# One semaphore for both scatters of a buffer, 30 loads in halves, and holes in two more groups of a rank-and-scatter kernel

## Chip, cores, metric

One core of one Trainium2 chip. The metric is the device time of one execution in microseconds (us). The kernel before took 771.68 us at first (median of 3 runs, 771.5 to 772.51). A change counts as faster or slower from 2% on. Chips differ at this size: on some the kernel before took 771 to 798 us. They are called busy below, though what disturbs them is not known, and their runs are marked.

## The reference

```python
B, N, D = 8, 2048, 2560
order = np.argsort(scores, axis=1)
ranks = np.argsort(order, axis=1)
out[b_idx, ranks, :] = x          # float32, each row of 10240 bytes goes to the place of its rank
```

## The kernel before

VectorE counts for each score how many are smaller; that is the rank. The rest is moving 168 MB in and 168 MB out. Each batch has 8 groups of 256 rows. Group 0 of the first six batches is copied row by row from DRAM to DRAM by the two hardware queues, issued from SyncE (SP) and ScalarE (ACT): "hardware rows". The other 58 groups are loaded by GpSimd into one of 8 buffers (128 partitions, two rows each) and written by two indirect scatters, one for each column of rows.

A set of four neighbouring partitions is served by one of the 16 DMA engines. In some groups a set of four is left out (a "hole"): its rank is pushed out of bounds so that the scatter skips it, and its rows go as hardware rows instead. That relieves one engine.

```python
NBUF, LAG, G = 8, 4, 16
DIRECT = range(6)
THIN = {**{(b, 4): 48 for b in range(1, B, 2)}, (7, 5): 44}   # (batch, group): first partition of the hole
THIN_LOADS = [k for k in THIN if k[0]]                         # these loads skip the hole as well
HALVED = range(34)                                             # loads 0..33 are issued as two halves
... # cut
def load(line, k, sem):
    ... # cut: groups of THIN_LOADS use an indirect load that skips the hole
    for j in range(m if k in HALVED else 1):
        part = slice(j * D, (j + 1) * D) if k in HALVED else slice(0, m * D)
        line.eng.dma_start(out=xb[k % NBUF][:, part], in_=rows[:, part]).then_inc(sem, 16)
... # cut
def scatters_done(line, k):
    i = k % NBUF
    for j in range(GROUPS[BULK[k][1]][1]):
        line.wait(s_scat[i][j], 16 * n_scat[i][j])
... # cut
for k, (b, g) in enumerate(BULK):
    if k >= LAG and k + NBUF - LAG < len(BULK):
        scatters_done(pl, k - LAG)
        load_ahead(k + NBUF - LAG)
    pl.wait(*loaded[k])
    pl.after(dve, t_bulk[b, g])
    for j in range(GROUPS[g][1]):
        scatter(k, j)
```

## Time and profile before

| | before |
|---|---|
| span of the profiled execution | 769.8 us |
| HBM read, written | 168.25 MB, 168.18 MB |
| data moved by the DMA engines | 415 GB/s mean |
| scatters, loads issued by GpSimd | 116, 62 halves + 21 whole + 5 with a hole |
| hardware rows | 792 (SP) + 784 (ACT) |
| end of the last 640-byte record on the hardware queues (SP, ACT) | 756.6 and 751.7 us |
| last landing (semaphore increment) of a scatter | 768.6 us |

In the profile's queue lists, q0 is GpSimd's queue, q1 and q10 are those of SP and ACT. The numbers behind a queue are records ("packets"), MB, and the share of 16 engines' time. A hardware row is one record of 640 bytes and one of 4 bytes (the semaphore) on each of the 16 engines.

### The profile page before, as it was taken

Reading aid. Unit: us, or ns where it says so; the run is one execution under the profiler, and the core shown is the slowest. Engines: PE = TensorE matmul, PEld = TensorE weight load, DVE = VectorE, ACT = ScalarE, POOL = GpSimd, SP = SyncE. Lnnn points to the kernel's source line nnn. Section 1 sums busy time; section 2 is a strip of 40 time slices with the busy share of each in tenths; the row PEclk is TensorE's granted clock in tenths of the full one; section 3 lists DMA queues with packets and bytes.
Section 4 is the critical chain, followed back from the end, with each engine's and each line's share of the span. In section 5 each row is a group of like instructions: output and inputs, shape, how many; then the busy total and the mean of one; then the engine's idle time right before and its main releaser. Section 6 shows DMA issues by size and latency. Waiting matters only on the chain.

```text
span 769.8 us, 8160 instructions
## 1 busy us (share of the span) xinstructions
PE 33.4 (4%) x166; PEld 29.2 (4%) x166; DVE 400.1 (52%) x824; ACT 0.0 (0%) x1; POOL 167.1 (22%) x213
## 2 busy tenths in 40 slices
PE   4000020020020020110000000000000000000000
PEld 4000010010010010110000000000000000000000
DVE  5999979999979999899999200000000000000000
ACT  0000000000000000000000000000000000000000
POOL 4114214312213131221212121212112121312100
PEclk8555555555555555565555555555555555555555
DMA  8999999999999999999999999999999999999997
GB/s 356 420 419 418 418 421 417 417 419 419 418 417 417 416 419 417 419 419 418 417 418 418 425 417 423 417 422 419 422 417 423 419 420 422 419 425 416 426 411 332
DMA packets 80130, 319.74 MB, mean 415 GB/s; under 512 B 28580, under 2 KB 53796, under 8 KB 53796
## 3 DMA queue, kind: packets, MB, share of 16 engines
q0 software_dynamic: 29376, 300.66, 92.0%
q1 hardware_dynamic: 25648, 10.85, 5.2%
q10 hardware_dynamic: 25088, 8.08, 4.2%
q14 instruction: 17, 0.14, 0.0%
q8 instruction: 1, 0.02, 0.0%
HBM read 168.25 MB, written 168.18 MB: 437 GB/s over the span
## 4 chain that ended last, share of the span: by engine, by line
DMA 63%; DVE 13%; another core or an unknown queue 10%; POOL 6%; issue 4%; PE 1%; POOLq 0%; SPq 0%
DMA out_dram<-x,rank_i 57%; DVE trash L262 12%; DMA x<-in_x_dram 6%; POOL out_dram L476 4%; POOL x L149 2%; DVE s_all L384 0%; POOL x L135 0%; PE ps_all L219 0%; DMA s_in<-in_scores_dram 0%; PE ps_col L198 0%; DVE rank_i L300 0%; DVE rank L294 0%; DVE rank L288 0%; PE ps_row L323 0%
## 5 line engine op out<-in xcount | busy, mean ns | idle before, releaser
L262 DVE TENSOR_SCALAR_CACHE_REDUCE trash<-s_all,s_col 128x1792 bf16<-128x1792 f32 (+7 forms) x240 | 315.2, 1348 | 4.6
L476 POOL DMA_INDIRECT out_dram<-x,rank_i x116 | 113.4, 978 | 135.8 <-issue 34.3
L149 POOL DMA_DIRECT2D x<-in_x_dram x83 | 46.7, 564 | 393.3 <-DMA out_dram<-x,rank_i 391.3
L262 DVE SCALAR_TENSOR_TENSOR trash<-s_all,s_col,mask 128x256 bf16<-128x256 f32 x128 | 61.5, 481 | 0.0
L219 PE MATMUL ps_all<-ident,s_col 128*128 128x128 f32 x128 | 27.2, 400 | 3.2 <-DVE s_all L384 2.8
L219 PEld LDWEIGHTS ps_all<-ident,s_col 128*128 128x128 f32 x128 | 26.0, 219 | 4.1 <-DVE s_all L384 3.1
L323 PE MATMUL ps_row<-ident,rank 128*1 128x128 f32 x22 | 5.9, 365 | 388.7 <-DVE rank_i L309 281.5
L384 DVE COPY s_all<-ps_all 128x512 f32<-128x512 f32 x32 | 20.6, 687 | 3.2 <-PE ps_all L219 2.8
L262 DVE DVE_READ_ACCUMULATOR trash<-s_all,s_col 128x1 f32 x240 | 19.9, 83 | 0.0
L323 PEld LDWEIGHTS ps_row<-ident,rank 128*1 128x1 f32 x22 | 1.3, 86 | 391.5 <-DVE rank_i L309 282.8
L135 POOL DMA_INDIRECT x<-in_x_dram,thin_row x5 | 5.2, 1031 | 43.9 <-DMA out_dram<-x,rank_i 40.3
L262 DVE DVE_READ_ACCUMULATOR trash<-s_all,s_col,mask 128x1 f32 x128 | 10.7, 83 | 0.0
L334 DVE TENSOR_SCALAR thin_i<-ps_row 1x8 int32<-1x8 f32 x5 | 0.8, 153 | 10.2 <-PE ps_row L323 10.2
L349 DVE TENSOR_SCALAR rows_i<-ps_row 1x256 int32<-1x256 f32 x6 | 2.5, 412 | 4.1 <-PE ps_row L323 4.1
L206 DVE COPY s_col<-ps_col 128x128 f32<-128x128 f32 x1 | 0.3, 292 | 4.5 <-PE ps_col L198 4.5
L198 PE MATMUL ps_col<-ident,s_in 8*128 8x8 f32 x16 | 2.1, 262 | 3.7 <-DMA s_in<-in_scores_dram 3.7
L198 PEld LDWEIGHTS ps_col<-ident,s_in 8*128 8x128 f32 x16 | 2.0, 211 | 3.7 <-DMA s_in<-in_scores_dram 3.7
L300 DVE CAST rank_i<-rank 128x16 int32<-128x16 f32 (+3 forms) x11 | 1.9, 173 | 0.4
L294 DVE TENSOR_TENSOR rank<-rank,acc 128x16 f32<-128x16 f32 (+3 forms) x11 | 1.9, 171 | 0.4
L288 DVE TENSOR_TENSOR rank<-acc,acc 128x16 f32<-128x16 f32 (+3 forms) x11 | 1.9, 170 | 0.4
L309 DVE TENSOR_SCALAR rank_i<-rank,hole 128x2 int32<-128x2 f32 x5 | 1.1, 229 | 0.2
L179 POOL TENSOR_SCALAR_AFFINE_SELECT mask<-mask 128x256 f32<-128x256 f32 x2 | 0.8, 396 | 0.0
(13 smaller groups left out, 2.5 us busy)
## 6 DMA issues: line engine op xcount, KB each, us to landing
x<-in_x_dram POOLq DMA_DIRECT2D x62, 1280.0 KB
x<-in_x_dram POOLq DMA_DIRECT2D x21, 2560.0 KB
out_dram<-in_x_dram SPq DMA_DIRECT2D x792, 10.0 KB
out_dram<-in_x_dram ACTq DMA_DIRECT2D x784, 10.0 KB
x<-in_x_dram SPq DMA_DIRECT2D x2, 1280.0 KB, 9.0
out_dram<-x,rank_i POOLq DMA_INDIRECT x116, 48.3
x<-in_x_dram,thin_row POOLq DMA_INDIRECT x5
s_in<-in_scores_dram SPq DMA_DIRECT2D x1, 64.0 KB
```

The costliest lines, as they stand in the source:

```text
L135: nc.gpsimd.indirect_dma_start(out=xb[k % NBUF][:, :m * D], out_offset=None, in_=x.rearrange("b (q j) d -> (b q) (j d)", j=m), in_offset=b ...
L149: line.eng.dma_start(out=xb[k % NBUF][:, part], in_=rows[:, part]).then_inc(sem, 16)
L198: nc.tensor.transpose(out=ps_col[:, B * c:B * (c + 1)], in_=s_in[:, r + j:r + m * P:m], identity=ident[:B, :B],)
L219: nc.tensor.transpose(out=ps_all[:, P * c:P * (c + 1)], in_=s_col[:, c, b:b + 1].to_broadcast([P, P]), identity=ident[:],)
L262: do(out=trash[i][:, :P * (hi_c - lo_c)], in0=s_all[:, P * lo_c:P * hi_c], accum_out=acc[i][:, col:col + 1], **how,)
L288: nc.vector.tensor_tensor(out=rank[:, cols], in0=acc[0][:, cols], in1=acc[1][:, cols], op=OP.add)
L294: nc.vector.tensor_tensor(out=rank[:, cols], in0=rank[:, cols], in1=acc[2][:, cols], op=OP.add)
L300: nc.vector.tensor_copy(out=rank_i[:, cols], in_=rank[:, cols])
L323: nc.tensor.transpose(out=ps_row[:1, P * j:P * (j + 1)], in_=rank[:, col:col + 1], identity=ident[:],)
L349: nc.vector.tensor_scalar(out=rows_i[b][:].rearrange("o (p j) -> o p j", p=P), in0=ps_row[:1, :WIDE].rearrange("o (j p) -> o p j", p=P), s ...
L384: nc.vector.tensor_copy(out=s_all[:, 512 * q:512 * (q + 1)], in_=ps_all[:, 512 * q:512 * (q + 1)],)
L476: nc.gpsimd.indirect_dma_start(out=out_flat, out_offset=bass.IndirectOffsetOnAxis(ap=rank_i[:, col:col + 1], axis=0), in_=xb[k % NBUF][:, ...
```

## The change

The aim, as the edit suggests it, is balance at the end. Two groups more get a hole: one column of (4,4) skips partitions 48-51, both columns of (6,4) skip 36-39; their loads stay whole. Four loads fewer are cut in halves, and one semaphore counts both scatters of a buffer, which saves half of the waits.

```diff
-    THIN = {**{(b, 4): 48 for b in range(1, B, 2)}, (7, 5): 44}
+    THIN = {(1, 4): 48, (3, 4): 48, (4, 4): 48, (5, 4): 48, (6, 4): 36, (7, 4): 48, (7, 5): 44}
+    THIN_COLS = {k: 1 if k == (4, 4) else 2 for k in THIN}
-    THIN_LOADS = [k for k in THIN if k[0]]
-    HALVED = range(34)
+    THIN_LOADS = [(1, 4), (3, 4), (5, 4), (7, 4), (7, 5)]
+    HALVED = range(30)
...
-        s_scat = [[nc.alloc_semaphore(f"scat{i}_{j}") for j in range(MMAX)] for i in range(NBUF)]
+        s_scat = [nc.alloc_semaphore(f"scat{i}") for i in range(NBUF)]
...
         def scatters_done(line, k):
-            i = k % NBUF
-            for j in range(GROUPS[BULK[k][1]][1]):
-                line.wait(s_scat[i][j], 16 * n_scat[i][j])
+            line.wait(s_scat[k % NBUF], 16 * n_scat[k % NBUF])
... (ranks pushed out of bounds, rows copied and scatters bounds-checked for THIN_COLS columns, not for all)
```

More of the change, by code (lines that the diff above doesn't have):

```diff
@@ L97 @@
     thin_row = pool.tile([P, len(HOLES)], I32, name="thin_row")
-    thin_i = {k: pool.tile([1, 4 * MMAX], I32, name=f"thin_i{k[0]}_{k[1]}") for k in THIN}
+    thin_i = {k: pool.tile([1, 4 * THIN_COLS[k]], I32, name=f"thin_i{k[0]}_{k[1]}") for k in THIN}
     rows_i = {b: pool.tile([1, WIDE], I32, name=f"rows_i{b}") for b in DIRECT}
@@ L117 @@
         s_load = [nc.alloc_semaphore(f"load{i}") for i in range(NBUF)]
-        s_scat = [
-            [nc.alloc_semaphore(f"scat{i}_{j}") for j in range(MMAX)]
-            for i in range(NBUF)
-        ]
+        s_scat = [nc.alloc_semaphore(f"scat{i}") for i in range(NBUF)]
         s_rows = {sp: nc.alloc_semaphore("rows_sp"), act: nc.alloc_semaphore("rows_act")}
-        n_scat = [[0] * MMAX for _ in range(NBUF)]
+        n_scat = [0] * NBUF
         n_load = [0] * NBUF
@@ L304, in ranks @@
                 if (b, g) in THIN:
-                    cols = slice(b * C + first_col(g), b * C + first_col(g + 1))
+                    cols = slice(b * C + first_col(g), b * C + first_col(g) + THIN_COLS[b, g])
                     i = HOLES.index(THIN[b, g])
@@ L330, in thin_to_bytes @@
         def thin_to_bytes(b, g):
-            m = GROUPS[g][1]
+            m = THIN_COLS[b, g]
             dve.after(pe, pe.n)
@@ L420, in thin_rows @@
             )
-            for i in range(4 * m):
+            for i in range(4 * THIN_COLS[b, g]):
                 row = b * N + r + (THIN[b, g] + i % 4) * m + i // 4
@@ L474, in scatter @@
             col = b * C + first_col(g) + j
-            n_scat[k % NBUF][j] += 1
+            n_scat[k % NBUF] += 1
             nc.gpsimd.indirect_dma_start(
@@ L481, in scatter @@
                 element_offset=b * N * D,
-                **(dict(bounds_check=N - 1, oob_is_err=False) if (b, g) in THIN else {}),
-            ).then_inc(s_scat[k % NBUF][j], 16)
+                **(dict(bounds_check=N - 1, oob_is_err=False) if j < THIN_COLS.get((b, g), 0) else {}),
+            ).then_inc(s_scat[k % NBUF], 16)
         def load_ahead(k):
```

## The prediction

> **What bounds the kernel now.** The page comes first, and of it the slices of the span, the DMA queues and the chain.
>
> ```profile
> DVE  5999979999979999899999200000000000000000
> ...
> DMA  8999999999999999999999999999999999999997
> GB/s 356 420 419 418 418 421 417 417 419 419 418 417 417 416 419 417 419 419 418 417 418 418 425 417 423 417 422 419 422 417 423 419 420 422 419 425 416 426 411 332
> ...
> q0 software_dynamic: 29376, 300.66, 92.0%
> q1 hardware_dynamic: 25648, 10.85, 5.2%
> q10 hardware_dynamic: 25088, 8.08, 4.2%
> ...
> DMA 63%; DVE 13%; another core or an unknown queue 10%; POOL 6%; issue 4%; PE 1%; POOLq 0%; SPq 0%
> ```
>
> The DMA engines are busy in every slice but the first and the last. VectorE, which computes the ranks, is done by 428 us, so nothing that it does later can hold the end. The shares of the queues add up to 101.4%: there is no idle time to fill in the middle. Counting the packet records of the trace that are in flight at each moment, I find 16 or more at every sampled moment from 30 to 745 us (mean 16.4 of 16 engines). So each engine works without a pause until its own list is empty, and the kernel ends when the engine with the longest list ends. The waits agree:
>
> ```profile
> POOL x L149 <- DMA out_dram<-x,rank_i: 391.3, 43, 11.1
> ```
>
> GpSimd, which issues the loads and scatters, idles about 10 us of each 13.1 us iteration for a scatter to land, always four iterations behind; its instructions are not the limit. The end is seen in the stretches:
>
> ```profile
> 740.00:750.00 10.00, 0.00 (x0) 0.00 (x0) 0.00 (x0) 0.00 (x0) 0.87 (x1) 0.50 1.02 413
> 750.00:760.00 10.00, 0.00 (x0) 0.00 (x0) 0.00 (x0) 0.00 (x0) 0.00 (x0) 0.50 1.02 424
> 760.00:770.00 10.00, 0.00 (x0) 0.00 (x0) 0.00 (x0) 0.00 (x0) 0.00 (x0) 0.50 0.57 240
> ```
>
> The last two columns are DMA share and GB/s. Until 760 us all engines are full, then they run dry one after the other. How unevenly is told by the 16 semaphore increments of the last scatter in the trace, one from each engine, in us of the span:
>
> ```
> 765.0 765.3 765.4 765.5 765.6 765.6 765.9 765.9 765.9 766.0 766.1 766.2 766.4 766.8 767.6 768.6
> ```
>
> Median 765.9, mean 766.0; one engine (call it B) is 2.7 us late, another (A) 1.7, the third last 0.9. Perfect balance would end at 766.0, which is 2.6 us, or 0.3%, better. That is the most that any rebalancing can give.
>
> **Who A and B are.** I took the same increments for each scatter through the run and the lag of the last two behind the median. With scatter pairs (batch, group) in order, first column of each: (6,4) 5.2 and 5.3; (6,7) 5.3 and 5.9; (7,0) 4.0 and 5.3; (7,1) 2.6 and 3.9; (7,3) 2.5 and 4.5; (7,5) 1.2 and 2.4; (7,7) 1.7 and 2.7. The load of (7,4), which skips partitions 48-51, is queued just ahead of scatter (7,0), and that of (7,5), which skips 44-47, ahead of (7,1). So the engine that falls from 6.3 (second column of (6,7)) to 4.0 is B, served by the hole at 48, and the one that falls from 5.3 to 2.6 a step later is A, served by the hole at 44. B is late by some 0.4 us more in each iteration and is pulled back at each odd batch; A grows to 5.3 us by 430 us and stays there.
>
> **What the Trainium skill says.** "DMA: Bandwidth & Descriptors", section "The descriptor swizzle", gives for a 128-partition transfer engine = 8*(partition>>6) + ((partition>>2)&7): four partitions of a hole belong to one engine, 48 to engine 4, 44 to engine 3, 36 to engine 1. The trace numbers no engines, but it agrees that one hole pulls back just one of 16. Section "Queues, rings and completion order" says that each engine goes round-robin between the queue rows that it has work for; the three busy queues and the absence of gaps agree. Section "Why a DMA increments its semaphore by 16 and not by 1" warns that two DMAs in flight on one semaphore let a partial count mislead. The new code waits only for the full sum of both scatters, so the wait ends at the same landing as the two waits before. Section "Where 436 GB/s comes from" puts the ceiling at 435 GB/s; here 10240 bytes in 385 ns on 16 engines are 426, and the slices show 416 to 426, so nothing but fewer or cheaper packets, or better balance, is left.
>
> **The change, part by part.** Durations are from the packet records of this trace: a 10240-byte packet 386 ns (mean), a 20480-byte one 761 ns, a 640-byte packet 32 ns and its semaphore write 9 ns.
>
> ```profile
> x<-in_x_dram POOLq DMA_DIRECT2D x62, 1280.0 KB
> x<-in_x_dram POOLq DMA_DIRECT2D x21, 2560.0 KB
> out_dram<-in_x_dram SPq DMA_DIRECT2D x792, 10.0 KB
> out_dram<-in_x_dram ACTq DMA_DIRECT2D x784, 10.0 KB
> ```
>
> 1. Halves, 34 to 30. Four loads change from two issues to one: 62 becomes 54, 21 becomes 25. GpSimd saves 4 x 0.56 us of issue, beside its waits: worth 0. On each engine 4 loads x 8 partitions x (2 x 386 - 761 = 11 ns) = 0.35 us, and 4 semaphore writes x 9 ns = 0.04: -0.39 us on every engine.
> 2. Rows by the hardware queues. (4,4) adds 4 rows and (6,4) adds 8: 796 on the first queue, 792 on the second. A row is 16 packets of 640 bytes, one on each engine: 12 x (32 + 9) = +0.49 us on every engine. The two new loads stay whole (they are not in the list of thinned loads), so the skipped rows are now read twice, 0.12 MB in 168.
> 3. Hole at 48 in one column of (4,4): engine B drops 4 packets x 386 = -1.54 us.
> 4. Hole at 36 in both columns of (6,4): its engine drops 8 packets x 386 = -3.09 us. It is neither A nor B by the identification above, so this should not move the end.
> 5. One semaphore for two scatters: one wait instruction less for each buffer's turn, tens of ns on an engine that idles 391 us. Worth 0.
> 6. VectorE: one more reduction for the third hole (0.07 us) and two more pairs of small operations (0.23 us and 0.15 us each), early or done by 428 us: 0.
>
> Sum: an engine without a hole moves by +0.49 - 0.39 = +0.10 us. A ends at 767.6 + 0.1 = 767.7; B at 768.6 + 0.1 - 1.5 = 767.2; the third at 766.9. The last landing goes from 768.6 (B) to 767.7 (A): -0.9 us. The timed result follows one for one: 771.68 - 0.9 = 770.8 us, a ratio of 0.9988.
>
> **Rivals.**
> (a) A takes over at more than its 1.7, or B's gain is eaten. B's lag in the (6,4) to (6,7) stretch stands close to the 5.3 at which A stays flat for 20 iterations. If 5.3 were a ceiling that the hardware sets for any late engine, B would be back at it before the last batch and the 1.5 us would be lost: the end at 768.3 to 768.7, the time 771.4 to 771.8. Against it: B reaches 6.3.
> (b) The hole at 36 does serve one of the late engines, because indirect scatters map partitions otherwise or because I swapped engines. If A gets the 3.1 us, the end is B's, 767.2, or the third's, 766.9: 770.0 to 770.3. The author's choice of 36 speaks for it, the fall of A at the load with the hole at 44 against.
> (c) The longer list of hardware rows becomes the bound. The hardware queues' last packets end at 757.0 and 752.1; at about 0.9 us a row of one queue, four and eight rows more end near 761 and 759, six us ahead of the end. Unlikely; it would show as a tail of 640-byte packets and cost up to 1 us.
> (d) Whole loads give the hardware queues fewer turns. Against it: stretches with whole loads (500 to 700 us) move 420 to 421 GB/s, those with halves (200 to 400 us) 418. Part of that may be VectorE's end, which falls at the same place. If it is all the packets' doing, the gain of point 1 is 0.3 us for four iterations of 13.1 us (0.6%), the size that I have.
>
> **Range and chances.** The sum is -0.9, the rivals span -1.7 to +0.3, and the three runs of before lie 1.0 us apart, so a median can be off by some 0.5. I take 770.8 with 769.8 to 771.9. Two per cent are 15.4 us, six times the whole imbalance: within 2% is all but sure.
>
> **What would show it.** Right: 54 half and 25 whole loads, 796 and 792 rows; last landings with the latest engine 1.5 to 2 us behind the median instead of 2.7; from scatter (4,4) on, B 1.5 us less late than before; the median of the last scatter unchanged within 0.3 us. Wrong: if the late engine of the flat 5.3 drops by 3 at scatter (6,4), the hole at 36 serves A, and rival (b) holds; if B stands as late as before by (6,7), rival (a); if the median itself moved by over 0.5 us, the packet sums miss something, such as a changed rate of the hardware queues.

## The result, and the profile after

772.35 us (median of 4 runs, 771.57 to 772.64) against 771.59 us (4 runs, 771.11 to 772.51) of the kernel before. The ratio is 1.0007, 95% interval 0.999 to 1.0024. (A ratio is the mean time of one kernel's fast runs over that of the other's of the same rounds, so not quite the ratio of the medians.) So nothing measurable came of the change, and the 0.9 us that was predicted did not come. The median lies 0.45 us above the range. A second set (e4 below) gave 771.6 us and ratio 1.0006.

The page of the kernel after, the lines that answer to those of before:

```profile
DMA  8999999999999999999999999999999999999997
GB/s 358 419 419 420 418 419 418 419 418 416 420 416 418 418 411 420 419 418 418 423 418 420 423 416 425 415 427 416 425 416 425 418 424 414 426 415 422 419 414 311
...
q0 software_dynamic: 28800, 300.54, 91.9%
q1 hardware_dynamic: 25776, 10.89, 5.2%
q10 hardware_dynamic: 25344, 8.16, 4.2%
...
x<-in_x_dram POOLq DMA_DIRECT2D x54, 1280.0 KB
x<-in_x_dram POOLq DMA_DIRECT2D x25, 2560.0 KB
out_dram<-in_x_dram SPq DMA_DIRECT2D x796, 10.0 KB
out_dram<-in_x_dram ACTq DMA_DIRECT2D x792, 10.0 KB
```

The counts of loads and rows are those predicted. The shares of the queues are unchanged to 0.1%. Of the chain that ended last, named DMAs hold 44% in place of 63%. Nothing is read from that: a second profile of the same kernel (e4) has 63% again. The waits of GpSimd for scatters and the stretches at the end:

```profile
POOL x L148 <- DMA out_dram<-x,rank_i: 390.6, 43, 10.6
```

```profile
740.00:750.00 10.00, 0.00 (x0) 0.00 (x0) 0.00 (x0) 0.00 (x0) 0.00 (x0) 0.50 1.04 417
750.00:760.00 10.00, 0.00 (x0) 0.00 (x0) 0.00 (x0) 0.00 (x0) 0.00 (x0) 0.50 1.03 417
760.00:770.00 10.00, 0.00 (x0) 0.00 (x0) 0.00 (x0) 0.00 (x0) 0.00 (x0) 0.50 0.58 236
```

Both look as before: the same wait, engines full until 760 us. What differs is seen when the DMA queues are listed for the end alone, 755 to 771 us. First the kernel before, then the kernel after:

```profile
q0 software_dynamic: 505, 4.51, 66.5%
q1 hardware_dynamic: 54, 0.02, 0.4%
```

```profile
q0 software_dynamic: 474, 4.20, 62.1%
q1 hardware_dynamic: 453, 0.14, 3.6%
q10 hardware_dynamic: 376, 0.12, 3.0%
```

Before, hardware rows were practically over by then. After, they run to the very end: their last 640-byte records end at 767.7 and 766.1 us in place of 756.6 and 751.7. I had predicted 761 and 759 (counted to the last semaphore record, 0.4 us later). Eleven and fourteen us later than before is much more than the four and eight rows that were added.

**Where the rows' delay comes from.** The queues from 500 to 700 us, where all loads but those with a hole are whole, in the kernel before:

```profile
q0 software_dynamic: 6622, 79.81, 93.7%
q1 hardware_dynamic: 6623, 2.13, 4.3%
q10 hardware_dynamic: 6622, 2.13, 4.3%
```

The three record counts are equal. That is what comes out if each engine serves one record of each queue in turn, whatever its size: a 20480-byte piece of a load, a 640-byte piece of a row and a 4-byte semaphore write each take one turn. An iteration with a whole load has 8 + 1 + 2 x (8 + 1) = 27 records of q0 on an engine. So each hardware queue gets 27 turns, which is 13.5 rows, and both together 27 rows in 13.1 us, or 82.4 in 40 us; the trace has 82.8. With halves an iteration has 36 records of q0. There the counts are not equal, as the same list shows for 140 to 340 us:

```profile
q0 software_dynamic: 8563, 79.04, 93.4%
q10 hardware_dynamic: 7067, 2.28, 4.6%
q1 hardware_dynamic: 7004, 2.25, 4.5%
```

There, turns are not what limits the rows: 88 in 40 us, 92 from 390 to 430 us. What does limit them there is not known. A load turned whole thus costs the hardware queues turns. In the kernel after, the equal counts begin four iterations earlier (1321, 1314 and 1322 records from 380 to 420 us).

**The late engine.** The 16 last semaphore records of GpSimd's queue show the scatter side alone. In the kernel before they end at a median of 765.5 us, the latest at 768.1, 2.6 us behind. After: median 765.7, latest 768.9, 3.2 behind. (The last landing, the semaphore increment, comes 0.5 us later: 768.6 and 769.4.) The records of 10240 bytes show why one engine is late. Nearly all take 385 ns. After 430 us, 350 take 388 to 449 ns (mean 409), no two of them at the same time, which is what records of one engine would show; 25 iterations have 16 scatter records of an engine each, 400. So nearly every scatter record of one engine seems to be slow, while loads of 20480 bytes are not. And of the 375 records that start after the last 640-byte record has ended, only 1 is slow. After the change they stay slow until the hardware queues end 11 us later.

### The profile page after: what moved, and what is told of

It reads as the page before. It is cut to its first block, busy times and chain, and to the rows that moved or that the text cites. A ratio compares the mean times of both kernels' runs of the same rounds, so it can differ in the third digit from the quotient of the medians.

```text
span 770.6 us, 8145 instructions
## 1 busy us (share of the span) xinstructions
PE 34.4 (4%) x170; PEld 29.5 (4%) x170; DVE 400.8 (52%) x829; ACT 0.0 (0%) x1; POOL 164.8 (21%) x209
## 4 chain that ended last, share of the span: by engine, by line
DMA 44%; another core or an unknown queue 21%; DVE 13%; POOL 10%; issue 7%; PE 1%; POOLq 0%; SPq 0%
DMA out_dram<-x,rank_i 38%; DVE trash L261 12%; POOL out_dram L473 7%; DMA x<-in_x_dram 6%; POOL x L148 3%; PE ps_all L218 0%; DVE s_all L383 0%; DMA s_in<-in_scores_dram 0%; PE ps_col L197 0%; POOL x L134 0%; DVE rank_i L299 0%; DVE rank L293 0%; DVE rank L287 0%; PE ps_row L322 0%
## 5 line engine op out<-in xcount | busy, mean ns | idle before, releaser
L148 POOL DMA_DIRECT2D x<-in_x_dram x79 | 44.4, 564 | 390.6 <-DMA out_dram<-x,rank_i 390.6
L308 DVE TENSOR_SCALAR rank_i<-rank,hole 128x2 int32<-128x2 f32 (+1 forms) x7 | 1.6, 227 | 0.2
```

## The experiments

Theory L: whole loads and more rows make the hardware queues end late; one engine's scatters are slow as long as these queues run, and that engine's gain is spent there. Theory P: the packet sums of the prediction. The numbers that decide ("hw queues end" is the end of the last 640-byte record of SP's and of ACT's queue; scatter ends are those of the last 16 semaphore records of q0; slow records are those of 10240 bytes over 387 ns after 735 us; in time order of the runs):

```
kernel                       hw queues end   scatter end: median, latest, behind   slow   ratio to before
before                       756.6  751.7    765.5  768.1  2.6                      32
after                        767.7  766.1    765.7  768.9  3.2                      60    1.0007
e1  one semaphore            755.1  751.0    765.5  767.8  2.3                      38    0.9998
e2  30 halves                764.6  758.9    765.3  768.1  2.8                      61    1.0005
e3  both holes               764.8  757.0    765.9  767.9  2.0                      57    1.0002
e4  whole change again       766.5  764.1    765.7  768.1  2.4                      64    1.0006
e15 hole of (4,4) alone      759.0  757.4    766.8  767.5  0.7                      47    0.9988  (busy chip)
e16 hole of (6,4) alone      761.6  758.3    766.2  769.0  2.8                      51    1.0000  (busy chip)
e17 hole of (4,4) again      753.0  757.4    765.7  767.8  2.1                      38    0.9998
e18 both holes again         760.8  757.4    766.3  768.1  1.8                      52    1.0007
```

The intervals of e1 to e4, e17 and e18 are about 0.0013 wide to each side, so no ratio here is more than "same".

**e1.** Only `s_scat` and its counts as in the change.

> The kernel before with one semaphore for both scatters of a buffer and nothing else. Theory L (late rows: the four whole loads and the twelve extra rows make the hardware queues end about 11 us later, and one engine's scatters are slow as long as those queues run): no effect, ratio 1.000, hardware queues end at 757 and 752 us of the span as before, last landing within 0.3 us of 768.6. Rival S (the merged semaphore costs something, for example by holding back the reuse of a buffer): ratio 1.0005 to 1.001 and longer waits of GpSimd for scatters.

771.28 against 771.57 us, ratio 0.9998. Hardware queues end at 755.1 and 751.0. The semaphore is free, as both theories have it; rival S falls.

**e2.**

```diff
-    HALVED = range(34)
+    HALVED = range(30)
```

> The kernel before with 30 loads in halves in place of 34. Theory L: the hardware queues end some 3 to 5 us later (about 7 rows fewer served while four more loads are whole), the last landing stays within 0.4 us of 768.6 since packets saved (0.2 us an engine) and the slow packets added (0.2 us on one engine) cancel; ratio 0.9995 to 1.0005. Theory P (packet sums of the prediction): last landing -0.39 us, hardware queues unchanged.

771.89 against 771.57 us. The hardware queues end 8.0 and 7.2 us later, more than I expected, although no row was added. The queues from 380 to 420 us show why, first of the kernel before and then of e2:

```profile
q0 software_dynamic: 1725, 15.71, 92.8%
q1 hardware_dynamic: 1532, 0.49, 4.9%
q10 hardware_dynamic: 1531, 0.49, 4.9%
```

```profile
q0 software_dynamic: 1322, 16.01, 93.9%
q10 hardware_dynamic: 1322, 0.43, 4.3%
q1 hardware_dynamic: 1314, 0.42, 4.2%
```

The counts have become equal, and from 390 to 430 us the rows go at 81 per 40 us in place of 92. That is the turns at work. The latest engine is where it was, 768.1, so the 0.39 us of theory P is not seen. A part of that size was wrong from the start. At the end of the trace, where one engine works alone, a 385-ns record is followed by the next after 381 ns. So two halves take 762 ns. A whole piece lasts 761 ns; if it overlaps its neighbour by the same 4 ns, it takes 757, and 5 ns are saved, not 11. With the semaphore records that is an estimate of 0.18 us for four loads.

**e3.** The `THIN` part of the change without the rest.

> The kernel before with the two extra groups with holes (one column at 48, both columns at 36) and nothing else. Theory L: hardware queues end 5 to 7 us later (six rows each at 0.9 us or so), last landing near -0.9 us (late engine -1.6 for the hole, +0.4 for rows, +0.3 for slow packets), ratio 0.999. Theory P: -1.05 us in the same place (-1.54 + 0.49), and the 36 engine is not the last. If instead the last landing is at or above 768.6, the hole at 48 does not reach the late engine.

771.67 against 771.57 us. Hardware queues 8.2 and 5.3 us later. The latest engine moves by -0.2 us only; neither theory has that.

**e4.** The whole change.

> The changed kernel once more, on the chip of the three parts: ratio 1.0007 again within its interval, hardware queues end near 768 and 766 us, last landing 0.5 to 1 us later than that of the kernel before. If the difference of the first measurement was only noise of the runs: 0.9985 to 1.000.

771.6 against 771.57 us by medians, ratio 1.0006. Hardware queues end at 766.5 and 764.1, nearly as late as in the first profile. The latest engine is at 768.1, as in the kernel before, so the expected 0.5 to 1 us did not come, and 0.8 us earlier than in the first profile of the same kernel: so much do two profiles differ. The three parts' ratios add up to 1.0005, which agrees with the whole, within intervals that would hide twice that.

The next four fell on a busy chip (the kernel before 772 to 788 us there).

**e5.**

```diff
-    HALVED = range(30)      # the changed kernel
+    HALVED = range(58)
```

> The changed kernel with all its loads in halves. Theory L: hardware rows go at 89 per 40 us to the end instead of 83, so they end 20 to 30 us earlier than in the changed kernel (735 to 747 us), slow packets after 750 us of the span vanish, the late engine ends 1 us or less behind the median; but 28 loads more cost 45 ns each on every engine, 1.2 us, so the median of the last landings moves from 766 to about 767 and the time stays within 0.5 us of the changed kernel's. Theory P: hardware rows end where they did, all landings move by +1.2 us.

772.67 us, ratio 0.9968 (0.9929 to 1.0006), same. The profile was slow: the hardware queues ended at 781.9 and 775.2, against the expectation. The latest scatter engine was 0.7 us behind.

**e6.**

```diff
-    DIRECT = range(6)       # the kernel before
+    DIRECT = range(0)
```

> The kernel before with no group copied by the hardware queues (only the 40 rows of the holes are left to them). A measurement of the slow packets by themselves. Theory L (one engine's scatter packets are slow only while the hardware queues run): of the packets of 10240 bytes over 387 ns there are a few tens in place of 835, in short groups where the 40 rows run; the engine of the hole at 48 is then early, not late. Rival (that engine is slow in itself, or by the descriptors that GpSimd writes): some 800 to 900 slow packets again. The time is no question here; by packets it should rise, since a row through the buffers takes two packets of 381 ns and one by the hardware queues 16 times 34 ns: 1536 rows x (762 - 544) ns / 16 = 21 us more.

794.99 us, ratio 1.0258 (1.0193 to 1.0324), some 20 us slower as expected. The page's queue list shows how little is left on q1 and q10:

```profile
q0 software_dynamic: 31968, 332.12, 98.7%
q1 hardware_dynamic: 1072, 2.93, 1.0%
q10 hardware_dynamic: 512, 0.16, 0.1%
```

After 430 us, when no hardware row is left, 3 of 8099 records of 10240 bytes take 388 to 449 ns, against 350 of 7146 in the kernel before. That is the clearest result: one engine's scatters are slow because the hardware queues run beside them, not in themselves. In the first 430 us over-long records did not become rare (I had expected a few tens over 387 ns; counted from 25 us on there were 1006), but those are single ones of up to a microsecond on this busy chip and, early on, ones that are 6 ns too long.

The increments of the scatters' semaphores in e6 also tell who the engines are (us from the median of the 16, first column of each pair):

```
scatter    (4,4)  (5,0)  (5,4)  (5,5)  (6,7)  (7,0)  (7,1)  (7,5)
earliest   -6.1   -9.2  -10.3  -11.8  -11.7  -14.7  -13.8  -16.8
latest      7.0    7.0    7.0    7.0    7.0    7.0    4.0    4.5
```

One engine is 3.0 us earlier from each load with a hole at 48 on (queued just ahead of (5,0) and (7,0); 4 x 761 ns), and 1.5 us from each scatter column with one. It is the engine that the kernel before has late, and here it is 16.8 us early, as expected. The latest engine falls by 3.0 us at the load with the hole at 44, just ahead of (7,1). And from (5,5) to (6,7), with no row beside them, none of the 16 distances from the median, in order, changes by more than 0.1 us: no lag grows, and no gain is lost.

**e7.**

```diff
-    HALVED = range(30)      # the changed kernel
+    HALVED = range(1)
```

> The changed kernel with only the very first load in halves. Theory L: hardware rows go at 83 per 40 us throughout in place of 88, some 40 to 50 rows are left over when the loads are done, the hardware queues end well after the scatters: last packet at 775 to 790 us of the span, the time 5 to 20 us longer (ratio 1.007 to 1.025), the scatters themselves some 1 to 5 us earlier. Theory P: each whole load saves 45 ns to 97 ns an engine: 29 loads, 1.3 to 2.8 us faster (ratio 0.9965 to 0.998).

782.16 us, ratio 1.0103 (1.005 to 1.0156): unclear by the 2% rule, but all of the interval lies above 1, where e5 and e8 have 0.997 on the same chip. Theory P, which has it faster, is refuted for this step. The scatters' latest record ends at 765.5 us, earlier than in any kernel above, but the hardware queues end at 774.7 and 772.7. Here is the stretch from 765 to 771 us (last two columns: DMA share, GB/s), and then the queues from 765 us on:

```profile
765.00:771.00 6.00, 0.00 (x0) 0.00 (x0) 0.00 (x0) 0.00 (x0) 0.00 (x0) 0.50 1.02 55
```

```profile
q1 hardware_dynamic: 708, 0.23, 28.5%
q10 hardware_dynamic: 453, 0.14, 21.2%
q0 software_dynamic: 2, 0.01, 0.2%
```

Engines are counted busy and move 55 GB/s: left-over rows, with nothing to hide them. Rows went at 81.8 per 40 us from 140 to 340 us, with equal counts (6600, 6594 and 6498 records). The changed kernel has 89 there on a quiet chip, but e8, with 30 halves on this chip, only 83.4, so this pair says little about the halves; e2 above, and e11 against e9 below, are the clean comparisons.

**e8.**

```diff
-    (6, 4): 36              # the changed kernel
+    (6, 4): 48
```

> The changed kernel with the hole of (6,4) at 48 in place of 36, both columns, so that the late engine drops 8 packets more (3.2 us). Theory L: the last landing is no longer that engine's; it ends level with the median or ahead, the last of the others ends near 766.8 to 767.2, so the span falls by 1 to 1.5 us against the changed kernel, ratio to before 0.998 to 0.999. If the late engine still stands 2 us behind, the identification of the hole with that engine is wrong.

772.79 us, ratio 0.9969 (0.9931 to 1.0008), same. The latest scatter engine is at 766.3, 1.3 us behind the median, as theory L expected for the scatters. But the hardware queues ended at 769.9, so they were last.

Four more, on another busy chip (the kernel before 771 to 798 us). **e9** is e8 again; **e10** has 38 halves in it; **e11** is e5 again; **e12** is the kernel before with one semaphore and the single extra hole `(6, 4): 48`.

> The changed kernel with the hole of (6,4) at 48 once more, since the chip of its first run was disturbed (the kernel before took 772 to 788 us there). Theory L: the late engine ends level with the others, the last landings of scatters near 766.5 to 767; the hardware queues, ending at 766 to 768, are then the last by a little, span 769 to 769.6, ratio 0.9985 to 1.000. Rival (the late engine regains its lag): last landing 768 to 769 with that engine alone behind.

> The same hole at 48, and 38 loads in halves in place of 30. Theory L: the hardware queues end 6 to 8 us earlier than with 30 halves (758 to 761), so neither they nor the late engine is last; eight more halved loads cost 0.36 us an engine; last landing 767 or below, span 768.2 to 769, ratio 0.998 to 0.9995, the best of all kernels here. Rival: no gain from an earlier end of the hardware queues, so that the halves cost only their 0.36 us and it is slower than the kernel with 30 halves.

> The changed kernel with all loads in halves once more, for a fast profile: hardware queues end at 735 to 750 us, no slow packets of 388 to 449 ns after that, the late engine at most 1 us behind the median, the median 1.2 us later than in the changed kernel (767), last landing 767.5 to 768.3, ratio 0.999 to 1.0005.

> The kernel before with one semaphore for both scatters and one more group with a hole, (6,4) at 48, 34 loads in halves, nothing else of the change. Theory L: hardware queues end at 758 to 763; the late engine drops 8 packets of about 0.4 us and gains 8 rows of 34 ns, net -2.9 us, so it ends ahead of engine A; last landing 767 or below, span 768.2 to 768.8, ratio 0.998 to 0.9993. Rival: the drop shows as 1 us or less, as for the hole of (4,4).

Ratios 1.0065, 0.9992, 1.0068 and 1.0000, all with intervals of 0.004 to 0.006 to each side and unclear by the 2% rule; those of e9 and e11 lie just above 1. The profiles of e10 and e12 fell in the slow state, those of e9 and e11 did not. The expectations on the hardware queues failed: they ended at 780.3, 780.2, 770.9 and 780.3 us. The scatters were about as expected, latest at 766.4, 766.8, 767.5 and 766.1. In e9, from 768 us on, only leftovers run:

```profile
768.00:782.00 14.00, 0.00 (x0) 0.00 (x0) 0.00 (x0) 0.00 (x0) 0.00 (x0) 0.50 0.07 12
```

On these chips rows went at 80 to 84 per 40 us already in the part with halves (140 to 340 us), and from there the turns of the whole loads do not let them catch up. Why they are slower there, these runs do not show. From 500 to 700 us e11, all halves, serves 89 rows per 40 us, and e9, whole loads on the same chip, 83: halves do give the rows more turns, as theory L had it. The fast profiles e8, e9 and e11 do show which list is last on such a chip: that of the hardware rows.

A third chip, less busy (the kernel before 772 to 780 us), **e15** and **e16** with one extra hole each, all else as before; **e13** and **e14** are e12 and e10 again.

> The kernel before with the hole at 48 in one column of (4,4) alone. Theory L: four rows more, hardware queues end 2 to 4 us later; the late engine's last landing falls by 1.6 for the hole, less 0.14 for the rows and 0.2 to 0.5 for slow packets: 0.9 to 1.3 us earlier than 768.6, so that A or it is last at 767.4 to 767.8; ratio 0.9985 to 0.9995. Rival (its lag closes up again whatever it drops): last landing 768.3 or later. Theory P: -1.4.

> The kernel before with the hole at 36 in both columns of (6,4) alone. Theory L: eight rows more, hardware queues end 4 to 6 us later, the late engine has no hole here and pays 0.27 us for rows and 0.2 to 0.4 us for slow packets: last landing 769.0 to 769.4, ratio 1.0005 to 1.001, the loss in the change. Rival (36 helps the last engine): last landing below 768.

> The same kernel as e12, for an undisturbed chip: hardware queues end at 758 to 763 us, no scatter engine over 1 us behind the median, last landing 767 or below, span 768.2 to 768.8, ratio 0.9975 to 0.999. If the hardware queues end at 775 to 780 again, as on the disturbed chip, the span is theirs plus 1 us, and it shows nothing of the hole but the missing straggler.

> The same kernel as e10, for an undisturbed chip: hardware queues end at 758 to 762 us, last landing 767 or below, span 768 to 769, ratio 0.9975 to 0.9995. Against e13 it has four more rows, a hole of four packets more and four more loads in halves: about level, within 0.4 us.

e15: 771.73 us, ratio 0.9988 (0.9951 to 1.0025), latest engine 0.7 us behind. e16 (the hole at 36 alone): 772.78 us, 1.0000, latest 2.8 behind, last landing 769.4 us as expected. So 36 does not serve the latest engine. The scatters' increments say whom it serves: from (6,3) to the second column of (6,4) the third latest engine falls from 3.6 to 1.2 us behind the median, while the second (4.7 and 5.2) and the latest (5.9 and 5.9) do not fall. e13: 771.24 us, 0.9986 (0.9949 to 1.0022), latest 1.3 behind, last landing 767.7. e14: 771.97 us, 0.998 (0.9951 to 1.001), 1.4 behind, last landing 768.8, later than expected. None is a proven gain.

e15 looked as if the hole at 48 had worked in full, against e3. So the last two ran on one quiet chip: **e17** is e15 again, **e18** is e3 again.

> The same kernel as e15. If its missing straggler was real: latest engine at most 1.3 us behind the median of the last scatter records, last landing 0.8 to 1.3 us earlier than in the kernel before (768.6 undisturbed), ratio 0.9985 to 0.9995. If it was the scatter between profiles: 1.8 to 2.8 us behind, ratio 0.9995 to 1.0005.

> The same kernel as e3. Theory L with additive parts: the eight rows of the second hole cost 0.27 us on every engine alike, so the latest engine stays at most 1.5 us behind the median, last landing 0.3 us later than in e17. Rival (the second hole, through later hardware queues, gives the late engine its lag back): 2 us or more behind again, last landing 0.8 us or more later than in e17.

e17: 771.46 us, ratio 0.9998, latest engine 2.1 us behind. e18: 772.29 us, 1.0007, 1.8 behind. So e15's missing straggler was not the hole's doing alone: on that chip the other engines ended late too, at a median of 766.8. On one chip the second hole raises the median of the scatter ends by 0.6 and the latest by 0.3 us; that is the size of the cost of its rows and no sign that it gives the lag back, but two single profiles differ by as much without cause.

What became of the hole at 48 can be followed by the increments of the loads' semaphores (us behind the median, the second latest engine up to (7,1), which by its growth is B) in e17, and in both profiles of the changed kernel:

```
load            before   e17    after   e4
(5,2)           2.8      2.4    2.3     2.0
(6,7)           4.7      3.5    3.6     2.7
(7,0)           4.7      4.2    4.3     3.7
(7,1)           5.3      4.3    5.1     4.3
(7,7), latest   4.6      3.8    4.6     3.6
last scatter    2.6      2.1    3.2     2.4
```

After the hole and up to (7,1) B is up to 1.2 us less late in e17, of the 1.6 that it had dropped, and at the end 0.5 is left. In the first profile of the changed kernel the 1.1 us of (6,7) are down to 0.2 at (7,1) and gone at the end; e4 keeps 1.0 at (7,1) and 0.2 at the end. In e6, without rows, a drop stays.

## Why the prediction was wrong

- **What bounds the kernel**: right in the main. The engines are full until 760 us, the end is that of the latest engine, and a balance of engines can give 2.6 us at most. That no single engine ever pauses does not follow from 16 records in flight, since records on one engine overlap (10240-byte records last 385 ns and follow each other every 381).
- **B is the engine of the hole at 48, A that of the hole at 44, 36 is neither**: right, shown by the steps of e6 and, for 36, of e16. Rival (b) falls by its own sign: the late engine of the flat 5.3 does not drop at scatter (6,4). "A" as the last one of the new kernel, at 767.7, was wrong: the last landings came at 769.4 and 768.6 (e4), from one engine that stood alone 3.2 and 2.4 us behind, most likely B. The second latest stood 1.5 to 1.7 us behind in e1, e2, e17 and in the kernel before, and 0.7 to 1.2 with the hole at 36. This suggests that 36 serves the second latest engine in the tail, so that this one is not the A of before, which both scatters of (7,5) pull back once more; it is not proven (e15, without a hole at 36, has 0.6).
- **Semaphore, VectorE: 0**: right (e1 for the semaphore).
- **"-1.54 us" for B**: this is the step that failed. I took it that what B drops at (4,4) reaches the end one for one. Slow records make the drop 4 x 405 = 1.6 us, yet on a quiet chip only 0.2 to 0.8 is seen at the end (2.6 behind before; e4 2.4, e17 2.1, e3 2.0, e18 1.8), and nothing in the first profile of the changed kernel (3.2). This is near rival (a), which I set aside with "B reaches 6.3". Kernels without this hole have 2.3 to 2.8 (e1, e2, before), so even the 0.5 is hardly clear of the scatter. That a drop stays without rows (e6) and shrinks beside them points to the rows. Records are not numbered by engine, so B's own list could not be summed, and how the rest is lost stays open.
- **"-0.39 us on every engine" for the halves**: not seen (e2: latest engine unchanged). 0.18 us is what the spacing of records allows, and the late end of the hardware queues keeps B slow for longer (61 slow records after 735 us in place of 32; at some 20 ns each about 0.6 us, an estimate).
- **"+0.49 us" for the rows**: of the right size. Taking 381, 757 and 6 ns for each record of q0 out of the 16 engines' time from 500 to 700 us leaves about 36 ns for each of the 6622 pieces of rows with its semaphore write, an estimate; 12 rows are then 0.43. e18 against e17 shows +0.3 for eight rows.
- **Hardware queues "near 761 and 759"** and **rival (d)**: wrong. The prediction cited the Trainium skill, "DMA: Bandwidth & Descriptors", section "Queues, rings and completion order", for the turns between queue rows, but took it as an explanation of why there are no gaps. It did not count the turns. The queues ended at 767.7 and 766.1 in the first profile, 766.5 and 764.1 in e4. I set (d) aside because stretches with whole loads move more GB/s. They do, but that speed goes to the loads; the rows are served more slowly and are left over.

With what was measured, and with the estimates above, the sum is -0.5 (hole) + 0.4 (rows) + 0 (halves) = -0.1 us, which is the "same" of both measurements. Differences of 0.8 us between profiles of one kernel (e4 and the first) are as large as everything summed here. So the +0.45 us by which the first median passed the range is not explained beyond that scatter. The -0.9 us was wrong; that the change is slower is not shown.

## What to carry to other kernels

When queues share the DMA engines, count turns as well as bytes: larger pieces in one queue save little time there and take turns from the others. Look which queue ends last and how far the others are from that end, for a rebalancing that moves work to a queue with 10 us to spare may use them up. And what an engine gains in the middle of a kernel need not arrive: check at the end, on a quiet chip and with a repeat, what is left of it.

## What the Trainium skill lacked or had wrong

- "DMA: Bandwidth & Descriptors", section "Queues, rings and completion order", says that an engine drains a packet of some 9 to 17 descriptors before it changes rows. Here the queues get equal numbers of recorded packets of any size, 4 to 20480 bytes, as if a turn were a single one: 6622, 6623 and 6622 records of three queues in 200 us. It does not say what follows, that larger pieces in one queue slow the rows of another (92 to 81 rows in 40 us, e2).
- The same page, section "Latency and other measured facts", says that engines 7 and 15 are usually slower and guesses at the descriptor rings of GpSimd's queue. Here one engine was slow, by its hole the one of partitions 48-51, engine 4 by the page's own formula (the trace numbers none, and that the slow records are this engine's is argued: it is late beside rows and early without them). It was slow only in scatters and only while hardware queues ran (409 against 385 ns; 350 of 7146 records, against 3 of 8099 with GpSimd's queue alone), so in this case the guess does not fit.
- No page has what one record costs beside its neighbours: 10240 bytes follow each other every 381 ns, 20480 bytes last 761 ns, a 640-byte piece of a row and its semaphore write take about 36 ns together (estimate above).
